# Three weight units by halves of the tokens instead of five or six, in a two-layer decoder trunk on one Trainium2 core

## The chip, the cores and the metric

The kernel runs on one core of one Trainium2 chip. A core has a matrix engine (TensorE, PE in the profile; its weight loads are PEld), a vector engine (VectorE, DVE), a scalar engine (ScalarE, ACT), GpSimd (POOL), and SyncE (SP), whose queue issues the DMAs here. The metric is the device time of one execution in microseconds; the median of the runs is given. Each engine works through its own list of instructions in order and waits on semaphores for the others.

## The reference

Two decoder layers over 512 tokens of width 1024, in float32. `swiglu_ffn` has hidden width 2816; the mixer has eight heads of windowed attention and eight of retention.

```
for l in range(DEPTH):
    x = layer_norm(ALPHA * x + 0.5 * swiglu_ffn(x, ffn1_w_gu[l], ffn1_w_down[l]), ln1_g[l], ln1_b[l])
    x = layer_norm(ALPHA * x + hybrid_mixer(x, w_in[l], w_out[l], attn_sinks[l], ...), ln2_g[l], ln2_b[l])
    x = layer_norm(ALPHA * x + 0.5 * swiglu_ffn(x, ffn2_w_gu[l], ffn2_w_down[l]), ln3_g[l], ln3_b[l])

def swiglu_ffn(x, w_gu, w_down):
    a, u = jnp.split(x @ w_gu, 2, axis=-1)
    return (jax.nn.silu(a) * u) @ w_down
```

So there are six stages in a row: block, mixer, block, block, mixer, block (a block is one SwiGLU with its layer norm). Each begins with matrix products whose input is the whole normalised x of the stage before.

## The kernel before

**Numbers in two parts.** Every float32 operand of a product is split into a high and a low part of the type fp32r (`split`, lines 153 to 158): ScalarE casts the high part (L154), VectorE subtracts it to get the low part (L155). A product is three matmuls (`mm3`, lines 160 to 165, the profile's L163, L164 and L165): high by high, high weights by low x, low weights by high x, added in one PSUM bank. PSUM has eight banks of 512 columns (`ps`), handed out in turn.

**Weights.** A weight unit is 128 output columns of a weight matrix, over all 1024 inputs. Its raw form comes by DMA, 1 MB for two units, into one of two buffers (`raw`), and is split into one of six unit buffers (`uh`, `ul`). The class `Weights` (lines 40 to 85) keeps a list of all units in order: `get` hands out the next one, `pump` loads and splits ahead as long as fewer than six unit buffers are out and no more than six units are ahead of those handed out, and `done` gives a buffer back.

**x transposed.** The products need x with its width on the partitions: `xh` and `xl`, 128 partitions by 8 chunks by 512 tokens. After a stage's last matmuls for a group of 128 tokens, `norm` (lines 401 to 425) does the layer norm of that group on VectorE (L408, L410, L417, L420), with one power on GpSimd (L416). It leaves a task in the list `pend`: eight transposes on TensorE (L385), two casts to `xh` on ScalarE and two subtractions to `xl` on VectorE (`to_xT`, lines 379 to 388). There are four groups, so four tasks. Group one is tokens 0 to 127, and so on; the program counts them from zero.

**Order of the work.** The program is a list in the order in which the Python code runs; a scheduler of the framework places the instructions of each engine, by that order and by when it reckons that inputs are ready. `keep_in_program_order` (line 157) pins the splits behind earlier work of their engine while `pin` is true, which it is until line 526. A task such as one in `pend` or `sums_of_x` is taken up when its due step comes (`step`, lines 125 to 129; `projs` makes a step after half a unit of 256 tokens, and two in a whole unit) or when `finish` is called on it. The delays after a block's norms are 4, 3, 9 and 9 steps (line 33) and after a mixer's always 4.

**The start of a stage.** When a stage begins, groups one and two of x are there, and three and four are still in the layer norm. So the first units are worked by halves: first columns 0 to 255 of the tokens for several units, then columns 256 to 511 for the same units. A half is 24 matmuls of 256 columns, a unit over all tokens 24 of 512.

In a block (lines 523 to 554), four units (a0, u0, a1, u1 of the first pair of column blocks) are worked on the first half, then `finish(self.pend[2:])` makes sure that groups three and four are transposed, then a fifth unit follows on the first half; then the second halves of the five. A sixth unit (u of the second pair) is also worked by halves, at line 548, and two more units over all tokens. `gate` (L513, L514) computes silu(a) times u into `hT`. `sums_of_x` (lines 442 to 456; L450, L454) prepares sums of x's quarters for the later column pairs 2 to 10, which use seven products of half size in place of eight.

In a mixer (lines 669 to 680), five units (k, v and the query units 0, 1, 2) are worked on the first half; group three is transposed before query unit 1 and group four before query unit 2. Then come the second halves of the five, and query unit 3 over all tokens. Each but v is rotated (`rotate`, lines 761 to 769): four copies on ScalarE (L766), two products (L767, L768) and a sum (L769).

Of the kernel before, what the change touches and what calls it, by code (L numbers as in the profile page):

```python
# [15 lines left out]
SEQ = 512  # L16
# [71 lines left out]
class Trunk:  # L88
# [342 lines left out]
    def ffn(self, g, b, out=None):  # L431
        nc, tc, W = self.nc, self.tc, self.W
        with ExitStack() as ctx:
# [8 lines left out]
            def sums_of_x():  # L442

                x = hT[:, NF - KC :, :]
                B = [[x[:, i * H : (i + 1) * H, j * 256 : (j + 1) * 256] for j in range(2)] for i in range(2)]
                for i in range(2):
                    ks = slice(i * H, (i + 1) * H)
                    for j in range(2):
                        ts = slice(j * 256, (j + 1) * 256)
                        nc.vector.tensor_add(B[i][j], self.xh[:, ks, ts].bitcast(F32), self.xl[:, ks, ts].bitcast(F32))  # L450
                        yield 1
                for i, (dst, p_, q_) in enumerate(((B[0][0], B[0][1], B[0][0]), (B[0][1], B[1][1], B[0][1]),
                                                   (B[1][1], B[1][1], B[0][0]), (B[1][0], B[1][0], B[1][1]))):
                    nc.vector.tensor_sub(dst, p_, q_)  # L454
                    self.split(Th[:, i], Tl[:, i], dst)
                    yield 1
# [46 lines left out]
            def glu7(fp):  # L503
                a, u22 = seven(W.get(), W.get, 0, None)
                nc.scalar.activation(a, a, AF.Silu)
                u, _ = seven(W.get(), W.get, 1, u22)
                W.done()
                nc.vector.scalar_tensor_tensor(out=hT[:, 2 * fp : 2 * fp + 2, :].rearrange("p f t -> p (f t)"), in0=u,
                                               scalar=0.5, in1=a, op0=ALU.mult, op1=ALU.mult)

            def gate(f, a, u, t0, t1):
                sa = gp.tile([P, 512], F32, tag="t2", name=self.nm("t2"), bufs=2)
                nc.scalar.activation(sa[:, : t1 - t0], a[:, : t1 - t0], AF.Silu)  # L513
                nc.vector.scalar_tensor_tensor(out=hT[:, f, t0:t1], in0=u[:, : t1 - t0], scalar=0.5,  # L514
                                               in1=sa[:, : t1 - t0], op0=ALU.mult, op1=ALU.mult)

            def glu(au, f, t0, t1):
                a, u = self.ps(), self.ps()
                self.projs(a[:, : t1 - t0], au[0], t0, t1)
                self.projs(u[:, : t1 - t0], au[1], t0, t1)  # L520
                gate(f, a, u, t0, t1)

            for fp in range(NFP):
                if fp == 0:
                    us = [W.get() for _ in range(6)]
                    self.pin = False
                    au = [us[0:2], us[2:4]]
                    self.finish(self.pend[:2])
                    more = []
                    for t0 in (0, 256):  # L530
                        for c in range(2):
                            glu(au[c], c, t0, t0 + 256)
                            if t0:
                                W.done(2)
                        self.finish(self.pend[2:])
                        if not t0:
                            xs = self.spawn(sums_of_x(), 1)
                        self.pend = []
                        more.append(self.ps())
                        self.projs(more[-1][:, :256], us[4], t0, t0 + 256)  # L540
                    W.done()
                    continue
                if fp == 1:
                    a1, u0 = us[5], W.get()
                    for i in range(2):
                        t0 = i * 256
                        u = self.ps()
                        self.projs(u[:, :256], u0, t0, t0 + 256)
                        gate(2, more[i], u, t0, t0 + 256)
                    W.done()  # L550
                    u1 = W.get()
                    glu((a1, u1), 3, 0, SEQ)
                    W.done(2)
                    continue
                if fp == NFP - 1:
                    early = W.take()
                    hv = [v.rearrange("p (f t) -> p f t", f=2) for v in early]
                    self.split(hv[0], hv[1], hT[:, 0:2, :])
                if fp in SEVEN:
                    self.finish([xs])  # L560
                    glu7(fp)
                    continue
                a0, a1, u0 = W.get(), W.get(), W.get()
                glu((a0, u0), fp * 2, 0, SEQ)
                W.done(2)
                u1 = W.get()
                glu((a1, u1), fp * 2 + 1, 0, SEQ)
                W.done(2)
# [21 lines left out]
            for f in range(NF - TAIL):  # L590
                if f == NF // 3:
                    gb = self.load_ln(pool, g, b)
                u, h = W.get(), ahead.pop(0)
# [8 lines left out]
            us = [W.get() for _ in range(TAIL)]  # L602
# [18 lines left out]
    def mixer(self, sinks, cst, g, b):  # L621
        nc, tc, W = self.nc, self.tc, self.W
        with ExitStack() as ctx:
# [3 lines left out]
            c = self.c  # L627

            def const(name, tag=None):
                ap = cst[name]  # L630
                c[name] = cp.tile(list(ap.shape), F32, tag=tag or name, name=self.nm(name))
                nc.sync.dma_start(c[name], ap)
# [20 lines left out]
            def emit_T(kind, u, t0, t1):  # L653
                n = t1 - t0
                b_ = self.ps()
                self.projs(b_[:, :n], u, t0, t1)
                C, S = c["ropeC"][:, t0:t1], c["ropeS"][:, t0:t1]
                if kind == "v":
                    nc.scalar.copy(vaT[:, t0:t1], b_[:, :n])
                    return  # L660
                r_ = self.tmp("rr", 10)
                self.rotate(r_[:, :n], b_, C, S, n)
                if kind == "k":
                    hi, lo = (x[:, t0:t1] for x in self.kT)
                else:
                    hi, lo = (x[:, kind % 2, t0:t1] for x in self.qT[kind // 2])
                self.split(hi, lo, r_[:, :n])

            first = [(kind, W.get()) for kind in ("k", "v", 0, 1, 2)]
            self.finish(self.pend[:2])  # L670
            for kind, u in first:
                if kind in (1, 2):
                    self.finish([self.pend[1 + kind]])
                emit_T(kind, u, 0, 256)
            self.pend = []
            for kind, u in first:
                emit_T(kind, u, 256, SEQ)
                W.done()
            emit_T(3, W.get(), 0, SEQ)
            W.done()  # L680
            const("retC", "cos")
            const("retS", "sin")
            b_ = self.ps()
# [5 lines left out]
            us = [W.get() for _ in range(4)]  # L689
# [21 lines left out]
            us = [W.get() for _ in range(4)]  # L711
# [285 lines left out]
```

## Time and profile before

| what | value |
|---|---|
| median of 3 runs | 1847.5 us (1847.25 to 1847.67) |
| the profiled execution's own time | 1847.64 us |
| its span, first to last instruction | 1845.9 us |
| TensorE busy | 1831.1 us (99%) |
| VectorE busy | 1325.5 us (72%) |
| ScalarE busy | 790.9 us (43%) |
| read from memory over the span | 180.92 MB, 99 GB/s with the writes |
| granted TensorE clock, mean | 0.999 |

A timeline row reads: start in us from the span's start, duration in us, engine, line, operation, what is written and read, shapes, how many instructions were merged; in brackets the idle time of that engine before it and what ended it. TensorE's matmuls are pipelined: the duration of a row is longer than its distance to the next row, so the cost of a run of matmuls is read from start to start.

### The profile page before, as it was taken

The page shows a single profiled execution, that of the slowest core. Times are in us where ns is not written, and L with a number is a line of the kernel's source. Part 1 is how long each engine was busy: PE and PEld are TensorE (multiplying, and loading weights), DVE is VectorE, ACT ScalarE, POOL GpSimd, SP SyncE. Part 2 cuts the span into 40 slices and gives each one's busy share as a digit, 9 for nine tenths or more (in the row PEclk, how much of TensorE's full clock was granted, in tenths as well). Part 3 has the DMA queues.
Part 4 walks back from the last instruction along what each step waited for, and adds up shares of the span by engine and source line. Part 5 has one row for each costly group of instructions (what it writes and reads, how often), then busy time and mean ns, then how long its engine had stood idle before and what let it go on. Part 6 is the DMA issues. An engine that isn't in the chain of part 4 may idle for free.

```text
span 1845.9 us, 28977 instructions
## 1 busy us (share of the span) xinstructions
PE 1831.1 (99%) x12170; PEld 1669.1 (90%) x12170; DVE 1325.5 (72%) x1830; ACT 790.9 (43%) x1211; POOL 84.9 (5%) x72
## 2 busy tenths in 40 slices
PE   9999999999999999999999999999999999999998
PEld 9999988897789999988899999888877899999886
DVE  7899844656768899854688998447567687998535
ACT  4444433178723444433234444332786233444330
POOL 0000000111110000000000000001111100000001
PEclk9999999999999999999999999999999999999999
DMA  5233244122122332343212323441233122233421
GB/s 183 92 103 126 92 143 154 61 84 87 51 92 69 103 104 92 113 147 129 92 47 94 113 92 115 137 143 58 80 92 92 46 92 92 92 124 105 137 92 46
DMA packets 136946, 184.87 MB, mean 100 GB/s; under 512 B 3952, under 2 KB 115312, under 8 KB 136816
## 3 DMA queue, kind: packets, MB, share of 16 engines
q1 hardware_dynamic: 136816, 183.03, 30.6%
q8 instruction: 95, 1.56, 0.4%
q14 instruction: 35, 0.29, 0.0%
HBM read 180.92 MB, written 2.10 MB: 99 GB/s over the span
## 4 chain that ended last, share of the span: by engine, by line
PE 92%; DVE 2%; issue 2%; ACT 1%; DMA 1%; POOL 0%; SPq 0%; POOLq 0%; DVEq 0%
PE ps L163 29%; PE ps L164 29%; PE ps L165 29%; PE ps L385 1%; DMA raw<-in_ffn_w_gu_dram 1%; PE ps L824 1%; ACT sw L766 1%; PE ps L838 0%; PE ps L816 0%; PE ps L876 0%; PE ps L789 0%; ACT b L808 0%; POOL sw L768 0%; DVE Y L420 0%; DVE b L155 0%
## 5 line engine op out<-in xcount | busy, mean ns | idle before, releaser
L163 PE MATMUL ps<-xh,uh 128*128 128x256 f32 (+1 forms) x1616 | 482.8, 299 | 0.5 <-ACT uh L154 0.5
L164 PE MATMUL ps<-xl,uh 128*128 128x256 f32 (+1 forms) x1616 | 479.9, 297 | 0.3 <-DVE xl L155 0.3
L165 PE MATMUL ps<-xh,ul 128*128 128x256 f32 (+1 forms) x1616 | 479.7, 297 | 0.3 <-DVE ul L155 0.2
L155 DVE TENSOR_TENSOR ul<-raw,uh 128x1024 fp32r<-128x1024 f32 (+1 forms) x333 | 346.6, 1055 | 132.0 <-ACT uh L154 130.1
L154 ACT CAST uh<-raw 128x1024 fp32r<-128x1024 f32 (+1 forms) x333 | 299.1, 915 | 306.5 <-PE ps L164 237.1
L163 PE MATMUL ps<-Th,uh 128*128 128x256 f32 x1152 | 326.0, 283 | 0.0
L164 PE MATMUL ps<-Tl,uh 128*128 128x256 f32 x1152 | 326.0, 283 | 0.0
L165 PE MATMUL ps<-Th,ul 128*128 128x256 f32 x1152 | 326.0, 283 | 0.0
L163 PEld LDWEIGHTS ps<-xh,uh 128*128 128x128 f32 x1616 | 309.2, 191 | 10.9 <-issue 1.6
L165 PEld LDWEIGHTS ps<-xh,ul 128*128 128x128 f32 x1616 | 309.1, 191 | 9.2 <-DVE ul L155 0.7
L164 PEld LDWEIGHTS ps<-xl,uh 128*128 128x128 f32 x1616 | 309.3, 191 | 8.4 <-DVE xl L155 0.6
L163 PE MATMUL ps<-uh,hh 128*128 128x512 f32 x640 | 249.5, 390 | 0.0
L165 PE MATMUL ps<-uh,hl 128*128 128x512 f32 x640 | 249.0, 389 | 0.0
L164 PE MATMUL ps<-ul,hh 128*128 128x512 f32 x640 | 249.0, 389 | 0.0
L163 PEld LDWEIGHTS ps<-Th,uh 128*128 128x128 f32 x1152 | 221.2, 192 | 0.0
L164 PEld LDWEIGHTS ps<-Tl,uh 128*128 128x128 f32 x1152 | 221.2, 192 | 0.0
L165 PEld LDWEIGHTS ps<-Th,ul 128*128 128x128 f32 x1152 | 221.2, 192 | 0.0
L154 ACT CAST uh<-S 128x1024 fp32r<-128x1024 f32 x144 | 151.2, 1050 | 132.0 <-PE ps L164 129.6
L155 DVE TENSOR_TENSOR ul<-S,uh 128x1024 fp32r<-128x1024 f32 x144 | 175.6, 1219 | 16.1 <-ACT uh L154 15.8
L155 DVE TENSOR_TENSOR hl<-hT,hh 128x512 fp32r<-128x512 f32 x80 | 54.3, 691 | 178.9 <-ACT hh L154 178.9
L154 ACT CAST hh<-hT 128x512 fp32r<-128x512 f32 x80 | 48.6, 622 | 222.1 <-PE ps L164 211.6
L163 PEld LDWEIGHTS ps<-uh,hh 128*128 128x128 f32 x640 | 120.1, 188 | 24.9
(128 smaller groups left out, 2273.0 us busy)
## 6 DMA issues: line engine op xcount, KB each, us to landing
raw<-in_ffn_w_gu_dram SPq DMA_DIRECT2D x86, 1024.0 KB, 5.1
raw<-in_ffn_w_down_dram SPq DMA_DIRECT2D x44, 1024.0 KB, 4.8
raw<-in_w_in_dram SPq DMA_DIRECT2D x18, 1024.0 KB, 5.3
raw<-in_w_in_dram SPq DMA_DIRECT2D x8, 512.0 KB, 5.0
raw<-in_w_out_dram SPq DMA_DIRECT2D x8, 512.0 KB, 5.7
raw<-in_w_out_dram SPq DMA_DIRECT2D x4, 1024.0 KB, 4.9
ln<-in_ln_g_dram SPq DMA_DIRECT2D x6, 512.0 KB, 4.3
ln<-in_ln_b_dram SPq DMA_DIRECT2D x6, 512.0 KB, 5.7
```

The costliest lines, as they stand in the source:

```text
L154: a = self.nc.scalar.copy(hi, src)
L155: b = self.nc.vector.tensor_sub(lo, src, hi.bitcast(F32))
L163: mm(out, ah, bh, start=start, stop=False)
L164: mm(out, ah, bl, start=False, stop=False)
L165: mm(out, al, bh, start=False, stop=stop)
L385: nc.tensor.transpose(b[:, c * P : (c + 1) * P], src[:, c * P : (c + 1) * P], self.ident)
L766: nc.scalar.copy(sw[q * 32 : q * 32 + 32, :n], src[o * 32 : o * 32 + 32, :n])
L824: mm(yb[cs, :], self.va[:, blk, cs], pT[kv][:, kb, :], start=kb == 0, stop=kb == nb - 1)
```

## The change

In a block, three units (a0, u0, a1) are worked by halves instead of six. Group three's transposes stand between the second unit and the third, group four's after the third; both halves of a unit go to one PSUM bank, and gates run over all 512 tokens. The fourth unit (u1) is worked over all tokens, and the second pair of column blocks (fp 1) takes the general path of lines 563 to 568, over all tokens. In the mixer, three units (k, v, query unit 0) are worked by halves, with the groups' transposes in the same places, and query units 1, 2 and 3 over all tokens.

```diff
             for fp in range(NFP):
                 if fp == 0:
-                    us = [W.get() for _ in range(6)]
+                    us = [W.get() for _ in range(4)]
                     self.pin = False
-                    au = [us[0:2], us[2:4]]
+                    banks = [self.ps() for _ in range(3)]
                     self.finish(self.pend[:2])
-                    more = []
                     for t0 in (0, 256):
-                        for c in range(2):
-                            glu(au[c], c, t0, t0 + 256)
+                        for i in range(3):
+                            if i == 2:
+                                self.finish(self.pend[2:3])
+                            self.projs(banks[i][:, t0 : t0 + 256], us[i], t0, t0 + 256)
                             if t0:
-                                W.done(2)
-                        self.finish(self.pend[2:])
+                                W.done()
+                            if t0 and i == 1:
+                                gate(0, banks[0], banks[1], 0, SEQ)
+                        self.finish(self.pend[3:])
                         if not t0:
                             xs = self.spawn(sums_of_x(), 1)
                         self.pend = []
-                        more.append(self.ps())
-                        self.projs(more[-1][:, :256], us[4], t0, t0 + 256)
+                    u1 = self.ps()
+                    self.projs(u1, us[3], 0, SEQ)
                     W.done()
-                    continue
-                if fp == 1:
-                    a1, u0 = us[5], W.get()
-                    for i in range(2):
-                        t0 = i * 256
-                        u = self.ps()
-                        self.projs(u[:, :256], u0, t0, t0 + 256)
-                        gate(2, more[i], u, t0, t0 + 256)
-                    W.done()
-                    u1 = W.get()
-                    glu((a1, u1), 3, 0, SEQ)
-                    W.done(2)
+                    gate(1, banks[2], u1, 0, SEQ)
                     continue
...
-            first = [(kind, W.get()) for kind in ("k", "v", 0, 1, 2)]
+            first = [(kind, W.get()) for kind in ("k", "v", 0)]
             self.finish(self.pend[:2])
             for kind, u in first:
-                if kind in (1, 2):
-                    self.finish([self.pend[1 + kind]])
+                if kind == 0:
+                    self.finish(self.pend[2:3])
                 emit_T(kind, u, 0, 256)
+            self.finish(self.pend[3:])
             self.pend = []
             for kind, u in first:
                 emit_T(kind, u, 256, SEQ)
                 W.done()
-            emit_T(3, W.get(), 0, SEQ)
-            W.done()
+            for kind in (1, 2, 3):
+                emit_T(kind, W.get(), 0, SEQ)
+                W.done()
```

## The prediction

> **What bounds the kernel now.** I read the page first, then TensorE's own timeline where a stage begins, then ScalarE's and VectorE's timelines at the same places.
>
> ```profile
> span 1845.9 us, 28977 instructions
> PE 1831.1 (99%) x12170; PEld 1669.1 (90%) x12170; DVE 1325.5 (72%) x1830; ACT 790.9 (43%) x1211; POOL 84.9 (5%) x72
> PEclk9999999999999999999999999999999999999999
> PE 92%; DVE 2%; issue 2%; ACT 1%; DMA 1%; POOL 0%; SPq 0%; POOLq 0%; DVEq 0%
> ```
>
> TensorE is busy for 99% of the span at full clock, and 92% of the chain that ended last is TensorE. So two things alone can move the time: how long TensorE needs for its instructions, and gaps in its stream. What a unit of weights (24 matmuls) costs is read from where one form follows the other, at the end of the first stage's halves:
>
> ```profile
> 43.84 0.28 PE L163 MATMUL ps<-xh,uh 128*128 128x256 f32 x1
> ...
> 46.72 0.40 PE L163 MATMUL ps<-xh,uh 128*128 128x512 f32 x1
> ...
> 52.18 0.39 PE L163 MATMUL ps<-xh,uh 128*128 128x512 f32 x1
> ```
>
> The first row begins the last half unit, the second the unit after it, the third the next. Half a unit takes 46.72 - 43.84 = 2.88 us (24 x 120 ns), a whole one 52.18 - 46.72 = 5.46 us (24 x 227 ns).
>
> **What the change removes.** Per unit run whole instead of by halves TensorE saves 2 x 2.88 - 5.46 = 0.30 us. The two SwiGLU blocks per layer go from six units by halves to three (12 units over the kernel), the two mixers from five to three (4 units): 16 x 0.30 = 4.8 us, all of it on TensorE and so on the path.
>
> The Trainium skill, page TensorE: Matmul & The Clock Gate, section Back-to-back issue gap, puts an isolated matmul at N / 2.4 + 2.5 ns, so that halving N costs 2.5 ns a pair and the removal would give an estimated 384 x 2.5 ns = 1.0 us. The trace has 13 ns a pair, and the measurement decides; by the page the forecast would be 3.8 us higher.
>
> **What it takes away: cover.** Each stage opens with halves because columns 256 to 511 of the transposed x (token groups three and four) are still to come: layer norm on VectorE, eight transposes on TensorE, two casts to `xh` on ScalarE, two subtractions to `xl` on VectorE. Before, a first half of some unit stood between the fourth group's transposes and the first matmul that reads these columns. Afterwards that matmul is the very next instruction: the order is unit, unit, group three, unit, group four, second halves. Everything else on TensorE reads all tokens, so there is nothing to fill in. Group three is still covered by the third unit's 2.88 us. The stage from one SwiGLU block to the next (layer 0 to 1) has the shortest queues:
>
> ```profile
> 924.97 0.28 PE L163 MATMUL ps<-xh,uh 128*128 128x256 f32 x1
> ...
> 936.48 1.91 PE L385 MATMUL ps<-ident,Y 128*128 128x128 f32 x16
> ...
> 941.10 0.28 PE L163 MATMUL ps<-xh,uh 128*128 128x256 f32 x1
> ...
> 931.02 1.28 DVE L420 SCALAR_TENSOR_TENSOR Y<-Y,rs,ln 128x1024 f32<-128x1024 f32 x1 [0.44 <-POOL rs L416]
> ...
> 937.73 2.48 DVE L155 TENSOR_TENSOR xl<-ps,xh 128x512 fp32r<-128x512 f32 x4 [0.55 <-ACT xh L154]
> ...
> 937.12 2.05 ACT L154 CAST xh<-ps 128x512 fp32r<-128x512 f32 x4 [2.93 <-PE ps L385]
> ```
>
> From the start T of a group's transposes the first cast begins 0.64 us later, the first subtraction 1.25 us later, and that one (2.48 / 4 = 0.62 us) ends at T + 1.87. The second matmul of a second half reads `xl`, so it starts at T + 1.9 at best. Eight transposes take TensorE 0.79 us (580.60 to 581.39, quoted next), so it would like to start that matmul at T + 0.91. **The floor is a stall of 1.0 us per stage**, six stages: 6.0 us, already a little more than the saving. What each stage adds to the floor:
>
> *Block to block (once).* T = 924.97 + 2 x 2.88 + 0.79 + 2.88 = 934.4, and the norm's last write (931.02 + 1.28 = 932.3) is done. Only a VectorE piece that happens to run can delay `xl`; the longest such pieces take 1.22 us (next fence). I take 1.3, between 1.0 and 2.2.
>
> *Mixer to block (twice).*
>
> ```profile
> 574.85 0.28 PE L163 MATMUL ps<-xh,uh 128*128 128x256 f32 x1
> ...
> 580.60 1.03 PE L385 MATMUL ps<-ident,Y 128*128 128x128 f32 x8
> 581.39 0.36 PE L163 MATMUL ps<-xh,uh 128*128 128x256 f32 x1
> ...
> 584.34 0.28 PE L163 MATMUL ps<-xh,uh 128*128 128x256 f32 x1
> ...
> 579.23 2.00 ACT L154 CAST uh<-raw 128x1024 fp32r<-128x1024 f32 x2 [5.85 <-DMA raw<-in_ffn_w_gu_dram]
> ...
> 584.52 1.28 DVE L420 SCALAR_TENSOR_TENSOR Y<-Y,rs,ln 128x1024 f32<-128x1024 f32 x1
> ...
> 586.64 1.22 DVE L450 TENSOR_TENSOR hT<-xh,xl 128x1024 f32<-128x1024 f32 x1
> ```
>
> Here group three already stands after two units, so TensorE's order is the old one until the third half ends at 584.34. Then group four is next, but its norm ends at 584.52 + 1.28 = 585.8: VectorE is late with it because the weight splits that follow the casts at 579.23 run between its steps. So 1.5 us of waiting for the norm, then the 1.0 of the floor: 2.5. The sum of x (L450), ready early, would start in the gap as it does at 586.64 and hold `xl` back by up to 0.8 more: 3.3. Were the splits put behind the norm, 1.0 is left. I take 2.9, near the top, since nothing in the change moves the splits.
>
> *Block to mixer (twice).* The same place in the mixer has ScalarE's rotary copies (L766) ahead of the casts:
>
> ```profile
> 360.56 0.28 PE L163 MATMUL ps<-xh,uh 128*128 128x256 f32 x1
> ...
> 369.20 1.04 PE L385 MATMUL ps<-ident,Y 128*128 128x128 f32 x8
> 369.99 0.36 PE L163 MATMUL ps<-xh,uh 128*128 128x256 f32 x1
> ...
> 369.39 0.74 ACT L766 COPY sw<-ps 32x256 f32<-32x256 f32 x2 [1.51 <-PE ps L165]
> 370.64 0.41 ACT L154 CAST qk<-rr 128x256 fp32r<-128x256 f32 x1 [0.51 <-DVE rr L769]
> 371.07 0.74 ACT L766 COPY sw<-ps 32x256 f32<-32x256 f32 x2
> 371.83 1.07 ACT L154 CAST xh<-ps 128x512 fp32r<-128x512 f32 x2
> ...
> 368.74 0.42 DVE L767 TENSOR_TENSOR rr<-ps,ropeC 128x256 f32<-128x256 f32 x1 [2.84 <-DMA ropeC<-c_ropeC_dram]
> ...
> 372.45 0.69 DVE L155 TENSOR_TENSOR xl<-ps,xh 128x512 fp32r<-128x512 f32 x1 [0.19 <-ACT xh L154]
> ```
>
> In this trace group three, transposed at 369.20, has its first `xl` at 372.45 + 0.69 = 373.14, T + 3.94: four copies of unit 0 and the cast of k, late because the rotary table lands at 368.74, stand in front. Afterwards group four is transposed at 360.56 + 2 x 2.88 + 0.79 + 2.88 = 370.0, behind the same unit 0, with the same copies and perhaps the same cast ahead of it. With T + 3.94 the stall is 3.94 - 0.91 = 3.0 us. With the copies alone (0.2 + 1.48 + 0.54 + 0.07 + 0.62 = 2.9) it is 2.0; with the casts let past them, the floor. I take 2.6.
>
> *The first stage (once).*
>
> ```profile
> 15.30 0.28 PE L163 MATMUL ps<-xh,uh 128*128 128x256 f32 x1
> ...
> 22.73 0.36 PE L163 MATMUL ps<-xh,uh 128*128 128x256 f32 x1
> ...
> 26.04 0.28 PE L163 MATMUL ps<-xh,uh 128*128 128x256 f32 x1
> 26.58 0.38 PE L164 MATMUL ps<-xl,uh 128*128 128x256 f32 x1 [0.26 <-DVE xl L155]
> ...
> 20.94 2.00 ACT L154 CAST uh<-raw 128x1024 fp32r<-128x1024 f32 x2 [2.18 <-DMA raw<-in_ffn_w_gu_dram]
> 22.84 2.04 ACT L154 CAST xh<-ps 128x512 fp32r<-128x512 f32 x4
> ...
> 24.65 2.48 DVE L155 TENSOR_TENSOR xl<-ps,xh 128x512 fp32r<-128x512 f32 x4
> ```
> ```profile
> L906 SPq DMA_DIRECT2D Y<-in_x_dram x2: 433/1084/1736, 8.1 to 9.8; - x2
> DMA to landing us min/median/max: 6.2/6.5/6.8
> ```
>
> Groups three and four of x were issued at 8.1 and 9.8 and land by 14.9 and 16.0, before they are wanted at 15.30 and 15.30 + 0.79 + 2.88 = 18.97. So the floor, 1.0. Two small stalls go: the fifth unit by halves took 26.04 - 22.73 = 3.31 instead of 2.88, and `xl` came 0.42 late at 26.58; together 0.85 us, as the fifth unit now comes over 10 us later and its data with room.
>
> **Edits at nothing.** Per block six gates of 256 columns and one of 512 become four of 512.
>
> ```profile
> L513 ACT ACTIVATE t<-ps x28: 370/378/591, 15.9 to 1532.1; 128x256 f32<-128x256 f32 x24, 128x512 f32<-128x512 f32 x4
> ```
>
> ScalarE's part goes from 6 x 0.378 + 0.591 = 2.86 to 2.36 us, under TensorE's matmuls; without that cover it would be a gain of 0.5. The mixer's rotations of units 1 and 2 merge likewise. Six weight buffers are filled ahead either way and are given back one by one from the second halves on. No DMA is added; the moved transposes issue none.
>
> **The sum.** Stalls 1.0 + 1.3 + 2 x 2.9 + 2 x 2.6 = 13.3; gains 4.8 + 0.85 = 5.7; net +7.6 us. The profiled execution took 1847.64 us (span 1845.9), which gives 1855.2; the median of the runs, 1847.5, lies 0.14 below, so **1855.1 us**, slower by 0.4%.
>
> **Rivals.** *Empty queues:* all six stalls are at the floor: 6.0 - 5.7 = +0.3, 1847.8. For it: at 936.48 the queues were empty. Against: the norm at 585.8 and the copies at 369.39 are there in the trace. 0.15.
>
> *The front queue (0.20):* the casts of the fifth and sixth weight units keep their place ahead of `xh` in the first stage. ScalarE then waits for the weights until 20.94, and `xl` ends at 24.65 + 0.62 = 25.27 instead of 20.8: a stall of 25.3 - 19.9 = 5.4 rather than 1.0, 1859.5. For it: that was the order before; against: group four is ready about 2 us sooner than then. The Trainium skill (same page, section Part 1: The HAM clock gate) says an idle window of about 3.4 us halves the clock until the array has been busy as long; an estimate of 1.7 us more, 1861. No gap in this trace is long enough to show it.
>
> *The other side (0.08):* instruction order is planned, and the planner puts group four's transposes ahead of the third unit, which then covers them as before. No stall is added: 1847.5 - 5.7 = 1841.8. It decides wherever group four's norm ends before the second unit does; in the block-to-block stage it ends at 932.3, after the second unit (930.7), and the transposes ran exactly where the program writes them in every stage quoted (after two, three and four halves). So little speaks for it.
>
> **From cases to numbers.** The forecast has 0.57, with 1851 to 1858 as its own range. From 1847 to 1861 leave out the other side and the far end of the front queue, about 0.15. A change under 0.2% (3.7 us) can't be told from none: slower, the forecast and the front queue, 0.75; same, the floors and the edge of the forecast, 0.18; faster 0.07.
>
> **What would show it.** By line, the matmuls of 256 columns that read `xh` go from 1408 to 1152 and those of 512 from 208 to 336. The second matmul of each stage's first second half waits for `xl`, about 1 us in the two quiet stages and 2 to 3 in the four others, and in the mixer-to-block stages the fourth group's transposes wait for L420. The forecast is wrong if that matmul follows without a gap, if the transposes stand ahead of the third unit, or if the new 512-column matmuls are not issued every 227 ns.

## The result: slower by 0.7%

The changed kernel takes 1860.6 us (median of 6 runs, 1859.43 to 1860.95), the kernel before 1847.75 us (6 runs, 1847.25 to 1848.28): a ratio of 1.0068, with 95% interval [1.0057, 1.0079]. The forecast was 1855.1 in a range of 1847.0 to 1861.0. The profiled execution took 1860.95 us with a span of 1859.2, so 13.3 us more than the profiled span before, where +7.6 was forecast.

Three views of the changed kernel answer to those shown of before. From the page:

```profile
span 1859.2 us, 28108 instructions
PE 1833.3 (99%) x11786; PEld 1654.8 (89%) x11786; DVE 1325.4 (71%) x1806; ACT 786.5 (42%) x1179; POOL 84.1 (5%) x68
PEclk9999999999999999999999999999999999999999
```

384 matmuls fewer, and yet TensorE is busy 2 us longer. The counts of line 163 are those that the prediction named (1152 matmuls of 256 columns on `xh` and 336 of 512). The waits say what is new (engine, line, what it waited for, us in all, times, longest):

```profile
PE ps L163 <- ACT xh L154: 5.4, 6, 2.2
PE ps L385 <- DMA Y<-in_x_dram: 3.5, 2, 3.4
PE ps L385 <- DVE Y L420: 3.1, 2, 1.6
```

That is 12.0 us of waiting in three kinds, none of which the kernel before had for more than 0.2 us. The stages follow from the view by windows: each from its first matmul on x to a matmul that both kernels have (the first on the sums of x in a block, the first token product in a mixer), in the order first block, mixer, block, block, mixer, block. Columns: window, length in us, busy us of PE, PEld, DVE, ACT and POOL with instructions, granted TensorE clock, DMA share, GB/s. The kernel before:

```profile
8.13:60.50 52.37, 51.29 (x379) 48.57 (x378) 43.84 (x54) 24.84 (x34) 0.00 (x0) 1.00 0.52 163
360.56:397.10 36.54, 36.54 (x286) 35.38 (x284) 22.93 (x43) 23.56 (x53) 7.49 (x9) 1.00 0.26 81
574.85:624.90 50.05, 50.05 (x377) 48.15 (x376) 44.53 (x56) 19.08 (x27) 2.46 (x2) 1.00 0.39 127
924.97:975.03 50.06, 50.06 (x377) 48.16 (x376) 40.39 (x52) 17.08 (x25) 1.45 (x1) 1.00 0.20 64
1275.10:1311.67 36.57, 36.57 (x285) 35.37 (x284) 22.93 (x43) 23.56 (x53) 7.41 (x9) 1.00 0.26 80
1489.43:1539.49 50.06, 50.06 (x378) 48.16 (x376) 44.46 (x56) 19.29 (x27) 2.48 (x2) 1.00 0.38 126
```

The changed kernel:

```profile
8.06:65.00 56.94, 52.94 (x307) 47.39 (x306) 44.24 (x51) 24.65 (x31) 0.00 (x0) 0.94 0.48 150
365.07:404.71 39.64, 37.48 (x237) 34.34 (x236) 21.66 (x36) 20.92 (x41) 7.08 (x7) 0.96 0.25 75
582.49:634.03 51.54, 49.68 (x305) 44.37 (x304) 44.44 (x53) 18.87 (x24) 2.47 (x2) 1.00 0.38 123
934.10:983.85 49.75, 49.51 (x306) 44.36 (x305) 40.26 (x49) 16.78 (x22) 1.45 (x1) 1.00 0.20 64
1283.91:1323.64 39.73, 37.49 (x237) 34.24 (x236) 21.66 (x36) 20.94 (x41) 7.00 (x7) 0.96 0.24 74
1501.45:1552.79 51.34, 49.66 (x305) 44.36 (x304) 44.44 (x53) 19.00 (x24) 2.46 (x2) 1.00 0.38 123
```

The differences are +4.57, +3.10, +1.49, -0.31, +3.16 and +1.28: together 13.3, all of the change. Only the block-to-block stage gained. In three stages the clock is no longer 1.00.

TensorE's timeline of the changed kernel where it stands still: the first stage, the first mixer, the block after it, and the block-to-block stage.

```profile
10.98 0.28 PE L164 MATMUL ps<-xl,uh 128*128 128x256 f32 x1
14.62 0.66 PE L385 MATMUL ps<-ident,Y 128*128 128x128 f32 x2 [3.36 <-DMA Y<-in_x_dram]
...
374.56 1.04 PE L385 MATMUL ps<-ident,Y 128*128 128x128 f32 x8
377.76 1.09 PE L163 MATMUL ps<-xh,uh 128*128 128x256 f32 x5 [2.16 <-ACT xh L154]
...
593.76 1.06 PE L385 MATMUL ps<-ident,Y 128*128 128x128 f32 x8 [1.62 <-DVE Y L420]
595.07 1.08 PE L163 MATMUL ps<-xh,uh 128*128 128x256 f32 x5 [0.24 <-ACT xh L154]
...
944.87 1.08 PE L163 MATMUL ps<-xh,uh 128*128 128x256 f32 x5 [0.24 <-ACT xh L154]
945.82 0.39 PE L164 MATMUL ps<-xl,uh 128*128 128x256 f32 x1
```

Two things in it were not foreseen. In the first stage two of group three's transposes stand inside the first half unit, after 14 of its 24 matmuls and the first two of the second unit's in the planned order, and wait for x. And after each group four five matmuls of line 163 stand in a row: the planner put the first matmul of five units together (the three second halves and two units over all tokens), because a unit's first product needs `xh` but not yet `xl`. The planned order of TensorE's instructions in the first mixer, as the built program has it, shows them:

```
L385 MATMUL ps_3653<-ident,Y 128x128 x4
L163 MATMUL ps_3660<-xh,uh_3254 128x256
L163 MATMUL ps_3702<-xh,uh_3289 128x256
L163 MATMUL ps_3732<-xh,uh_3301 128x256
L163 MATMUL ps_3774<-xh,uh_3308 128x512
L163 MATMUL ps_3814<-xh,uh_3312 128x512
L164 MATMUL ps_3660<-xl,uh_3254 128x256
```

### The profile page after: what moved, and what is told of

Its sections match the earlier page's. It is cut to its first block, busy times and chain, and to the rows that moved or that the text cites. A ratio compares the mean times of both kernels' runs of the same rounds, so it can differ in the third digit from the quotient of the medians.

```text
span 1859.2 us, 28108 instructions
## 1 busy us (share of the span) xinstructions
PE 1833.3 (99%) x11786; PEld 1654.8 (89%) x11786; DVE 1325.4 (71%) x1806; ACT 786.5 (42%) x1179; POOL 84.1 (5%) x68
## 5 line engine op out<-in xcount | busy, mean ns | idle before, releaser
L163 PE MATMUL ps<-xh,uh 128*128 128x256 f32 (+1 forms) x1488 | 459.2, 311 | 5.6 <-ACT xh L154 5.4
L165 PE MATMUL ps<-xh,ul 128*128 128x256 f32 (+1 forms) x1488 | 459.2, 309 | 0.2 <-DVE ul L155 0.2
L164 PE MATMUL ps<-xl,uh 128*128 128x256 f32 (+1 forms) x1488 | 458.9, 309 | 0.0
L163 PEld LDWEIGHTS ps<-xh,uh 128*128 128x128 f32 x1488 | 284.9, 193 | 22.0 <-ACT xh L154 6.8
L165 PEld LDWEIGHTS ps<-xh,ul 128*128 128x128 f32 x1488 | 286.8, 193 | 13.7 <-DVE ul L155 0.4
L164 PEld LDWEIGHTS ps<-xl,uh 128*128 128x128 f32 x1488 | 286.7, 193 | 13.8 <-DVE xl L155 0.9
L165 PEld LDWEIGHTS ps<-uh,hl 128*128 128x128 f32 x640 | 120.1, 188 | 25.0
```

The source lines that it names most:

```text
L163: mm(out, ah, bh, start=start, stop=False)
L164: mm(out, ah, bl, start=False, stop=False)
L165: mm(out, al, bh, start=False, stop=stop)
```

## The experiments

Every experiment was timed beside the kernel before on the same chip; "over before" is the difference of the medians there. The changed kernel is 12.85 over before.

### The first stage: the order of the transposes

```diff
+    def held(self, ins):
+        return self.tc.keep_in_program_order(ins) if self.pin_t else ins
...
-            nc.tensor.transpose(b[:, c * P : (c + 1) * P], src[:, c * P : (c + 1) * P], self.ident)
+            self.held(nc.tensor.transpose(b[:, c * P : (c + 1) * P], src[:, c * P : (c + 1) * P], self.ident))
```

`pin_t` is true for groups three and four of the first stage. Line numbers above 111 are one lower in this kernel.

> The transposes of groups three and four are held in program order in the first stage alone. Theory (a planned order): the changed kernel's first stage lost 4.5 us because two of group three's transposes stand inside the first unit and wait 3.4 us for x, after which the clock is half for 6.8 us. Held behind the second unit, where x has landed, the wait and the half clock go: 4 to 6 us less than the changed kernel's 1860.6, about 1855.5. Rival (x is simply late for three units): the wait moves to the transposes' new place and the time stays within 0.7 us of 1860.6.

Measured: 1856.9 against 1846.95, 9.95 over before, ratio 1.0051 [1.0036, 1.0066]: 2.9 us better than the changed kernel, less than the 4 to 6 expected. The wait for x is gone, but another took its place. TensorE and then ScalarE in this run:

```profile
18.69 1.04 PE L384 MATMUL ps<-ident,Y 128*128 128x128 f32 x8
21.87 1.43 PE L162 MATMUL ps<-xh,uh 128*128 128x256 f32 x4 [2.14 <-ACT xh L153]
...
19.34 1.99 ACT L153 CAST uh<-raw 128x1024 fp32r<-128x1024 f32 x2 [2.68 <-DMA raw<-in_ffn_w_gu_dram]
21.24 1.06 ACT L153 CAST xh<-ps 128x512 fp32r<-128x512 f32 x2
```

The casts of the fifth and sixth weight unit stand ahead of group four's, wait for their DMA until 19.34, and so `xh` comes at 21.24. Behind this gap of 2.14 us the granted clock is half for 3.4 us, and the stage takes 54.69 us. This is the front queue of the prediction, which the changed kernel itself didn't show: there the wait for x had come first.

### The first stage: the weights' casts

The same kernel, with the fifth and sixth unit split only behind group four (`W.cap` stops the pump after four units):

```diff
+                    W.cap = 4 if self.pin_t else None
                     us = [W.get() for _ in range(4)]
...
                         self.finish(self.pend[3:])
+                        if W.cap:
+                            W.cap, self.pin = None, True
+                            W.pump()
+                            self.pin = False
```

> As the run with the first stage's transposes held in order, and the casts of the fifth and sixth weight units stand behind group four's casts to xh. Theory (ScalarE's queue): the 2.3 us gap in which TensorE waits for xh behind two weight casts that wait for their DMA shrinks to the 0.4 us of the quiet stage, and the half clock of 3.4 us behind it goes: 3.6 us less than that run's 9.9 over the kernel before, so about 6.3 over it. Rival (xh is late for another reason): the gap stays, 9.5 to 10.3 over the kernel before.

Measured: 1853.01 against 1847.47, 5.5 over before, ratio 1.0029 [1.0018, 1.004]. ScalarE now has the order wanted, and TensorE waits 0.24 us:

```profile
19.64 1.07 ACT L153 CAST xh<-ps 128x512 fp32r<-128x512 f32 x2 [2.66 <-PE ps L384]
20.60 2.01 ACT L153 CAST uh<-raw 128x1024 fp32r<-128x1024 f32 x2
...
20.28 0.85 PE L162 MATMUL ps<-xh,uh 128*128 128x256 f32 x4 [0.24 <-ACT xh L153]
...
7.51:59.24 51.73, 50.16 (x305) 44.67 (x305) 43.83 (x51) 24.86 (x31) 0.00 (x0) 1.00 0.54 170
```

The first stage takes 51.73 us at full clock, 0.64 less than before and 5.2 less than in the changed kernel. So the loss there is the order of two queues, the transposes on TensorE and the casts on ScalarE, and not x landing too late for three units.

### The mixer: the gap filled with matmuls

```diff
             self.finish(self.pend[3:])
             self.pend = []
+            fill = self.ps()
+            for _ in range(20):
+                ins = nc.tensor.matmul(fill[:, :P], self.ident, self.ident, start=True, stop=True)
+                tc.keep_in_program_order(ins)
```

> Twenty matmuls of the identity by itself (20 x 0.109 = 2.2 us) stand behind group four's transposes in each mixer, where TensorE sat idle for 2.2 us; they compute nothing that is used. Theory (clock): the half clock of 3.4 us that follows the gap in each mixer goes, 2 x 1.7 = 3.4 us less; the four first matmuls of later units that were pulled into the gap go back to their units, 0.9 us more: about 1858. Rival (the slow stretch comes from waiting for xl or from the weights, not from the idle time): no gain, 1860.5 to 1862.

Measured: 1861.3 against 1846.95, 14.35 over before, ratio 1.0077 [1.0062, 1.0092]. As a test of the clock it failed: the size was wrong. Each of the twenty float32 matmuls is recorded twice, and together they took 4.4 us, twice the gap:

```profile
375.67 4.63 PE L671 MATMUL ps<-ident 128*128 128x128 f32 x40
380.05 0.36 PE L163 MATMUL ps<-xh,uh 128*128 128x256 f32 x1
```

The clock did stay full in both mixers of the profiled execution (40.17 us each at 1.00), but with the matmuls longer than the gap the time can't tell the theories apart. With ten in place of twenty:

> As the run with twenty dummy matmuls, with ten: each is recorded twice, so that twenty took 4.4 us and pushed the second halves back; ten take 2.2 us, the length of the gap. Theory (clock): no half clock in either mixer, each as long as the mixer without pulled matmuls whose clock stayed full (38.9 us, against 39.7 in the changed kernel): 1.5 us less than the changed kernel's 12.6 over the kernel before, about 11. Rival (the slow stretch doesn't come from the idle time): half clock in the mixers as before, 12.6 to 14 over it.

Measured: 1857.92 against 1846.78, 11.1 over before, ratio 1.006 [1.0044, 1.0077], where about 11 was expected. Both mixers:

```profile
363.98:402.78 38.80, 38.46 (x257) 35.20 (x256) 21.90 (x36) 20.86 (x41) 7.07 (x7) 1.00 0.24 76
1281.89:1320.52 38.63, 38.29 (x257) 35.18 (x256) 21.90 (x36) 20.86 (x41) 7.02 (x7) 1.00 0.23 76
```

Matmuls that compute nothing make each mixer about 1 us shorter than the 39.7 of the changed kernel: TensorE hardly stands still, and the clock stays at 1.00. The comparison has a second side: where the clock stayed full behind the gap by itself, as in the first mixer of the weights' casts experiment (window in the last section), the mixer took 38.08 us. So filling the gap costs 0.6 us and saves the 1.5 of the half clock.

### The mixer: cover

```diff
                 if kind == 0:
-                    self.finish(self.pend[2:3])
+                    self.finish(self.pend[2:])
                 emit_T(kind, u, 0, 256)
-            self.finish(self.pend[3:])
```

> In the mixers both groups are transposed between the second unit and the third, so that the third unit's first half covers the casts. Theory (cover): the gap of 2.2 us and the half clock behind it go, and what is left is the saving of two whole units: each mixer 3.1 + 0.6 = 3.7 us shorter, 1860.6 - 7.4 = 1853.2. Rival (the norm or ScalarE's queue is late anyway, as the copies of k and v and four casts now stand in a row): a gap of 1 to 2 us stays in each, 1855.5 to 1858.

Measured: 1852.89 against 1846.95, 5.9 over before, ratio 1.0031 [1.002, 1.0043]: 6.9 us better than the changed kernel. The mixers of this run:

```profile
363.98:400.04 36.06, 35.97 (x237) 32.88 (x236) 21.90 (x36) 20.66 (x41) 7.09 (x7) 1.00 0.26 82
1278.94:1314.94 36.00, 35.96 (x237) 32.88 (x236) 21.89 (x36) 20.70 (x41) 7.02 (x7) 1.00 0.26 82
```

Each is 0.5 us shorter than before the change, close to the 0.6 that two whole units save. With one half unit (2.88 us) between group four's transposes and their first reader the stall is gone; ScalarE's four casts in a row do no harm.

### The pulled matmuls

```diff
-        mm(out, ah, bh, start=start, stop=False)
+        ins = mm(out, ah, bh, start=start, stop=False); pin and self.tc.keep_in_program_order(ins)
```

`pin` holds for the first matmul of every unit that reads columns up to 511.

> The first matmul of each unit that reads columns up to 511 is held in program order, so none is pulled ahead. Theory (the filled gap): in the changed kernel TensorE does five such matmuls, 0.95 us of work, while xl is made; without the four of later units each of the six stages loses 0.45 to 0.69 us: 2.7 to 4.1 us more than 1860.6, about 1864. Rival (the start after the gap is set by xl in both, and the pulled matmuls give nothing): within 0.7 us of 1860.6.

Measured: 1863.36 against 1846.95, 16.4 over before, ratio 1.0089 [1.0072, 1.0106]: 3.6 more than the changed kernel. The block-to-block stage of this run, first on TensorE's timeline and then by its window:

```profile
944.41 0.38 PE L163 MATMUL ps<-xh,uh 128*128 128x256 f32 x1 [0.24 <-ACT xh L154]
945.36 0.39 PE L164 MATMUL ps<-xl,uh 128*128 128x256 f32 x1 [0.56 <-DVE xl L155]
...
933.64:984.07 50.43, 49.63 (x305) 44.49 (x304) 40.33 (x49) 16.89 (x22) 1.45 (x1) 1.00 0.19 64
```

With the order as written, the second matmul waits for `xl`, and the stage takes 50.43 us in place of 49.75. So the pulled matmuls are worth 0.7 us in this stage (0.5 to 0.8 in the four stages, the block-to-block stage among them, that have the same granted clock in both kernels), and the stall without them is 50.43 - 50.06 + 3 x 0.30 = 1.3 us.

### The block after a mixer: the weight splits

The changed kernel, with the two splits behind group four, by the `W.cap` edit above and this in the mixer's last lines:

```diff
                     half(t + 2, 0)
+            W.cap = W.taken + 4
             W.done(4)
```

> The changed kernel, where at the two stages from mixer to block the splits of the fifth and sixth weight unit stand behind group four's. Theory (VectorE's queue): these splits (2 x 1.2 us) run between the norm's steps and make L420 late; behind it, the transposes' wait of 1.6 us goes in both, 3.2 us less than the changed kernel's 12.6 over the kernel before, about 9.4 over it. Rival (the norm is paced by its own steps and the power on GpSimd): the wait stays, 12 to 13 over it.

Measured: 1856.88 against 1847.47, 9.4 over before, ratio 1.005 [1.0035, 1.0066]. TensorE at group four, and both stages:

```profile
591.87 1.06 PE L385 MATMUL ps<-ident,Y 128*128 128x128 f32 x8 [0.18 <-DVE Y L420]
...
582.04:632.15 50.11, 49.69 (x306) 44.42 (x305) 44.43 (x53) 19.01 (x24) 2.47 (x2) 1.00 0.38 126
1497.90:1548.01 50.11, 49.69 (x305) 44.42 (x304) 44.43 (x53) 18.94 (x24) 2.47 (x2) 1.00 0.38 126
```

The transposes' wait for L420 falls from 1.62 to 0.18 us, and the stage from 51.4 to 50.1. The norm was late because of the splits on VectorE. A stall of about 1.0 us (50.11 - 50.05 + 0.9) is left, so the stage only comes level with the kernel before.

### Cover kept: two kernels faster than before

Both take the mixer of the cover experiment, the changed block-to-block stage, and for the two blocks after a mixer the form of before with the sixth unit over all tokens:

```diff
                 if fp == 1 and self.five:
                     a1, u0 = us[5], W.get()
+                    u = self.ps()
+                    self.projs(u, u0, 0, SEQ)
                     for i in range(2):
-                        t0 = i * 256
-                        u = self.ps()
-                        self.projs(u[:, :256], u0, t0, t0 + 256)
-                        gate(2, more[i], u, t0, t0 + 256)
+                        gate(2, more[i], u[:, i * 256 :], i * 256, i * 256 + 256)
```

The first has this form in the first stage too; the second has the first stage of the weights' casts experiment.

> Each stage with the cover that its trace asks for: the first stage and the two from mixer to block as in the kernel before, but the sixth unit over all tokens; the block-to-block stage as changed; the mixers with both groups between the second and third unit. Theory, from stage lengths: 3 x 0.3 for the sixth units, 0.3 for block to block, 2 x 0.5 for the mixers: 2.2 us less than the kernel before. Rival (each edit moves the planner's order and makes a gap somewhere): no gain, or a loss of 1 to 3.

Measured: 1845.24 against 1847.47, ratio 0.9987 [0.9978, 0.9996]: 2.2 us faster, as expected.

> As the run with cover kept, but the first stage works three units by halves with its transposes held in order and the fifth and sixth unit's casts behind group four's. Theory: the first stage comes to about 51.1 us (52.4, less 0.9 for three whole units and 0.85 for two small stalls, plus a gap of 0.5), so 3.1 us less than the kernel before. Rival (x lands too late for three units, or a gap of 2 us stays and halves the clock): 1 to 2 us more than the kernel before.

Measured: 1844.03 against 1847.47, ratio 0.9982 [0.9973, 0.9991], 3.4 us faster than the kernel before, where 3.1 was expected. Its first four stages:

```profile
7.88:59.18 51.30, 50.23 (x307) 44.71 (x306) 43.89 (x51) 24.81 (x31) 0.00 (x0) 1.00 0.52 167
359.24:395.26 36.02, 35.98 (x237) 32.88 (x236) 21.88 (x36) 20.71 (x41) 7.09 (x7) 1.00 0.26 82
573.04:622.77 49.73, 49.73 (x354) 46.91 (x352) 44.45 (x56) 19.13 (x27) 2.47 (x2) 1.00 0.39 128
922.84:972.58 49.74, 49.50 (x306) 44.35 (x305) 40.25 (x49) 16.78 (x22) 1.45 (x1) 1.00 0.19 64
```

The last two take 36.01 and 49.73 us. All are shorter than before, the blocks after a mixer by the 0.3 of one unit. That the second kernel beats the first by 1.2 us is the difference of two medians, and the intervals of the ratios overlap; by windows its first stage is 0.5 us shorter (51.77 in the first kernel).

## Why the prediction was right or wrong

**The direction and its reason were right.** The saving is there: 0.30 us a unit shows in every stage whose cover was kept, and the six stages together hold the whole change. Behind the first stage, the stalls where cover was taken away come to 12.7 us, and the 13 units worked whole there give 3.9. The size was missed: 1860.6 lies above the forecast's own range of 1851 to 1858. That it lies within the wider one, whose upper end was the front queue with a half clock, is partly luck: what took it there was another mechanism, and misses of both signs elsewhere nearly cancel.

**By stage**, a stall being the stage's difference plus the units' saving (0.9 in a block, 0.6 in a mixer; in the first stage also the 0.85 of two small stalls):

| stage | stall forecast | measured | what the runs showed |
|---|---|---|---|
| first | 1.0 | 6.3 | transposes inside the first unit: 3.4 for the wait, 3.0 for the half clock |
| mixers | 2.6 each | 3.7, 3.8 | 2.2 as long as the clock stays full, 1.5 for the clock |
| blocks after a mixer | 2.9 each | 2.4, 2.2 | 1.6 for the norm, as forecast; then less |
| block to block | 1.3 | 0.6 | five matmuls pulled into the gap |
| sum | 13.3 | 19.0 | |

**The step that failed most is "The first stage (once)"**, which put the stall at its floor of 1.0 with the transposes where the program writes them. The term was 5.3 us too small. The miss in the span is 5.7, since the other three (2.3 too little for the mixers, 1.2 too much for the blocks after them, 0.7 too much for block to block) leave only 0.4. The landing of x was read rightly; the order wasn't. The planner moved two transposes of group three up, a move of the kind that the rival on the other side supposed for group four, but here it cost 3.36 us: x lands at about 14.6, and the place chosen comes up at 11.3. The clock was half from 13.83 to 20.65, and TensorE worked for 6.0 us of that, so 3.0 were lost. That the transposes "ran exactly where the program writes them in every stage quoted" was true of the kernel before and didn't carry over to a changed program. Why the changed program lets the planner do this and the program before did not is open; it wasn't tried. The front queue, whose 1859.5 (1861 with its clock) lies closest to the measured time, wasn't the mechanism of the changed kernel. It was real all the same: as soon as the transposes were held it made the gap of 2.14 us, and the first stage was 3.0 us longer with it and its half clock than without (54.69 against 51.73).

**"No gap in this trace is long enough to show it"** was where the clock was left out of the mixers. The Trainium skill (TensorE: Matmul & The Clock Gate, section Part 1: The HAM clock gate) asks for an idle window of about 3.4 us before the clock is halved, and I priced it for the front queue alone, so the mixers' term held nothing for the clock. In the changed kernel a gap of 2.16 us was enough. The stretch after the first mixer's gap and the stretch after that:

```profile
379.10:382.40 3.30, 3.30 (x17) 3.30 (x17) 0.60 (x2) 0.11 (x1) 0.00 (x0) 0.50 0.00 0
382.50:385.90 3.40, 3.40 (x30) 3.40 (x30) 1.51 (x2) 2.63 (x6) 0.24 (x1) 1.00 0.02 5
```

Seventeen matmuls in 3.3 us and then thirty in 3.4: half speed for a stretch, 1.5 us lost per mixer. The measured gap decides against taking the page's window as the shortest gap that matters; the last section shows when such a gap counts.

**"There is nothing to fill in" was wrong.** The floor of 1.0 a stage assumed that the second matmul waits for `xl` with TensorE idle. Holding the order as written gave 1.3 in the block-to-block stage, the size forecast; the planner's pulled matmuls brought it to 0.6. The floor was too high by that 0.7, and by 0.5 to 0.8 in the three other stages that can be compared. The sign of being wrong that the prediction named came with it: in the changed kernel no matmul waits for `xl` there, the first one waits 0.24 us or more for `xh`.

**Block after a mixer and block to mixer were right in mechanism.** The wait for L420 was put at 1.5 us a stage and measured 1.62 in the first of the two stages and 3.1 over both; the splits of the weights are its cause. In the mixer the copies and the cast of k stood ahead of `xh` as forecast: 2.2 against 2.6 without the clock.

## What to carry to other kernels

Work that looks like a plain loss, here a unit run by halves at 0.30 us more, may be the cover of a chain on other engines; before it is removed, the chain (transposes, casts, subtractions) is to be laid against what is left between its start and its first reader, stage by stage, since the queues differ in each. Moving the transposes one unit earlier in the mixers, or the weights' casts later in the first stage, kept the saving without the gap; in the blocks after a mixer later splits only brought the stage level. Where a scheduler may move instructions, one that waits for a DMA and comes to stand a unit earlier can block its engine until the data is there, as for 3.36 us here; the order is to be read from the changed program, not from the old one. And a gap on TensorE can cost more than its length, since half clock may follow it.

## What the runs showed of the hardware

The granted clock fell to half after idle gaps of 2.1 to 2.3 us, but not after each of them. Of ten such gaps before the second halves in the mixers, over the profiled executions of five kernels, five were followed by half clock and five not, with no order by length: 2.11 us (halved) and 2.33 us (not halved) both occur. The two mixers of one execution, by window (the weights' casts experiment), have the same work and nearly the same gap, 2.09 and 2.11 us:

```profile
359.31:397.39 38.08, 35.99 (x237) 32.85 (x236) 21.66 (x36) 20.90 (x41) 7.08 (x7) 1.00 0.24 78
1276.36:1315.97 39.61, 37.50 (x237) 34.26 (x236) 21.63 (x36) 20.90 (x41) 7.02 (x7) 0.96 0.24 74
```

38.08 us at full clock and 39.61 with the drop. What decides between them is the place of the gap in a period of 3.413 us. Within each of the eleven profiled executions, the changes of the granted clock in the trace all lie whole multiples of that apart: in the changed kernel at 7.00, 13.83, 20.65, 379.05, 382.46, 1297.24 and 1300.65 us. Cut into these periods, the gap of the first of the two mixers falls into two of them, and the other gap into one:

```profile
367.47:370.89 3.42, 2.37 (x21) 2.13 (x19) 1.96 (x6) 1.63 (x5) 0.75 (x1) 1.00 0.30 82
370.89:374.30 3.41, 2.37 (x18) 2.28 (x19) 2.38 (x5) 1.85 (x5) 0.72 (x1) 1.00 0.00 0
1285.66:1289.07 3.41, 1.30 (x12) 1.06 (x11) 1.45 (x5) 2.56 (x7) 0.92 (x2) 1.00 0.04 5
1289.07:1292.48 3.41, 3.41 (x14) 3.22 (x15) 1.86 (x4) 0.77 (x2) 0.07 (x1) 0.50 0.00 0
```

TensorE was idle for 1.05 and 1.04 us in the first two periods, and the clock stayed; it was idle for 2.11 us in the third, and the next was at half clock. Over all eleven executions, some 5900 periods, every period at full clock with at most 1.94 us of idle TensorE was followed by another at full clock, and every one with at least 1.98 us, 18 of them, by one at half. The clock came back after a half period without idle time; three half periods that held 0.79 to 1.72 us of it were followed by another. No run here moves a gap on purpose, so this rests on where the gaps happened to fall.

The gap of about 3.4 us in the first stage was followed by half clock in all six kernels that kept it: for 6.8 us in three, where it reached over the end of a period that was already idle enough, and for 3.4 us in the other three, where all but 0.3 us of it lay in one period.
